# FFN input projection: Strassen-Winograd products for 19 of 22 pairs of gate and value blocks

## The chip, the cores and the metric

One core of one Trainium2 chip runs the whole program. The metric is the device time of one execution in microseconds (us). Engines: TensorE (PE; PEld is its weight load), VectorE (DVE), ScalarE (ACT), GpSimd (POOL) and SyncE (SP, which here only issues DMAs). Each works through its own list of instructions in order and waits for the others by semaphores.

## The reference, cut to what matters

The program is one inference step of a 4-layer decoder: 512 prompt positions and 8 sample tokens, 520 columns in all, width 1024. Every layer has a token mixer (NSA, gMLP, HGRN2, NSA) and then a SwiGLU FFN with 2816 hidden units, 22 blocks of 128:

```python
def deepnorm(x, h, g, b):
    return layer_norm(DEEPNORM_ALPHA * x + h, g, b)
def swiglu_ffn(x, w_in, w_out):
    gate, up = jnp.split(x @ w_in, 2, axis=-1)
    return (jax.nn.silu(gate) * up) @ w_out
```

Everything is float32. The FFN runs four times, once in each layer, on all 520 columns.

## The kernel before, in words

Activations lie transposed: x is 8 blocks of 128 features by 520 columns (tile `x`). A matrix product in near-float32 is made of three matmuls. `Split.put` and `Weights.conv` cut an operand into a rounded high part (an ACT cast to fp32r, L101 for weights, L210 for activations) and a low remainder (a DVE subtraction, L102 and L211), and `mm` adds up H*a, L*a and H*b for each block k of 128 features (L249, L250, L251). Columns go in two halves of 256 and 264 (`HS`), one PSUM bank each.

The 22 pairs of an FFN (a gate block and a value block of 128 hidden units) go in three chunks of 8, 7 and 7 (`CH`). In `ffn`, each pair and half takes two `mm` of 8 blocks (gate, value), then silu on ACT (L419), the product with the value on DVE (L420), and the split of the result (L210, L211). In the first chunk of a layer the first three pairs run their first halves, then their second ones, while the layer norm of the second half still runs; the other 19 go pair by pair. After a chunk, `out_proj` multiplies its hidden units by w_out, in 8 blocks of two halves, and adds to `x` (L382, L384). The last chunk's sums (L361, L363 on POOL) feed the layer norm.

Weights stream in one planned order for the whole kernel: SP's DMAs (L88) run `rawn` units ahead of the conversion, and conversion runs `ahead` = 2 units ahead of the matmuls. A unit is one block of 128 x 1024 and is converted at once by `conv`: two ACT casts and two DVE subtractions of 512 columns (half of the subtractions go to POOL in NSA). All big tiles come from one pool of 38 slots (`g`). Nothing reorders the program: each engine's list is in the order in which the Python code emits instructions.

## Time and profile before

| what | value |
|---|---|
| median of 3 runs | 3082.68 us (3077.68 to 3083.25) |
| the profiled execution: its own time | 3078.4 us |
| its span, first to last instruction | 3076.7 us |
| mean granted TensorE clock | 0.976 of full speed |
| busy share of the span | PE 94%, PEld 90%, DVE 56%, ACT 42%, POOL 15% |

The page's second part cuts the span into 40 slices; the granted clock (PEclk) reads 9 in each, that is 90% or more of full speed. The page's chain of waits, followed back from the end, spends 34% on PE, of which three times 10% are the lines L249 to L251. Two facts are needed to read the rows below. Matmuls are pipelined, so a matmul of 281 to 284 ns starts about every 0.12 us, and the time of a product is counted by how far apart later events lie, not by adding the matmuls' lengths. And a timeline row merges neighbours of one kind ("x4"): its second number then runs from the first start to the last end.

### The profile page before, as it was taken

How to read it: one execution, taken by the hardware profiler on the slowest of the kernel's cores; microseconds unless marked ns; L12 is line 12 of the kernel's file. 1: busy time of each engine (PE TensorE's matmuls, PEld its weight loads, DVE VectorE, ACT ScalarE, POOL GpSimd, SP SyncE). 2: the span in 40 equal slices, each digit the busy share in tenths (PEclk: the TensorE clock that was granted, in tenths of full speed). 3: DMA queues.
4: the chain of work that ended last, by engine and by line, in shares of the span. 5: the costliest groups of instructions: out<-in, count | busy, mean ns of one | idle time of the engine just before them, and what ended most of it. 6: DMA issues, size and time to landing. Idle time of an engine off the chain costs nothing. (4 is left out here: it accounts for less than half of the span.)

```text
span 3076.7 us, 56298 instructions
## 1 busy us (share of the span) xinstructions
PE 2886.1 (94%) x22730; PEld 2759.4 (90%) x22730; DVE 1725.9 (56%) x3821; ACT 1293.8 (42%) x2902; POOL 473.4 (15%) x446
## 2 busy tenths in 40 slices
PE   8889889999989999999999999999988998899997
PEld 8888569999989899998899889999888876799997
DVE  4888655333566633337677773333668876533334
ACT  4666534222355432234445543122456665432322
POOL 0222141000031200004222230000312222400002
PEclk9999999999999999999999999999999999999999
DMA  5212532223223222322222223223222244233221
GB/s 173 69 59 80 165 124 90 96 77 108 71 83 97 76 90 92 101 89 71 78 71 73 76 100 94 94 80 95 81 87 63 63 155 130 97 97 94 85 86 40
DMA packets 136039, 280.61 MB, mean 91 GB/s; under 512 B 13026, under 2 KB 76002, under 8 KB 135778
## 3 DMA queue, kind: packets, MB, share of 16 engines
q1 hardware_dynamic: 127168, 261.86, 26.8%
q10 hardware_dynamic: 7458, 10.95, 1.0%
q0 software_dynamic: 1152, 4.19, 0.5%
q8 instruction: 179, 2.93, 0.4%
q14 instruction: 82, 0.67, 0.1%
HBM read 263.69 MB, written 13.27 MB: 90 GB/s over the span
## 5 line engine op out<-in xcount | busy, mean ns | idle before, releaser
L249 PE MATMUL ps<-g 128*128 128x256 f32 (+1 forms) x6176 | 1784.8, 289 | 19.5 <-ACT g L101 12.9
L250 PE MATMUL ps<-g 128*128 128x256 f32 (+1 forms) x6176 | 1758.0, 285 | 10.9 <-DVE g L102 5.8
L251 PE MATMUL ps<-g 128*128 128x256 f32 (+1 forms) x6176 | 1759.1, 285 | 3.0 <-DVE g L211 1.7
L249 PEld LDWEIGHTS ps<-g 128*128 128x128 f32 x6176 | 1180.2, 191 | 34.6 <-ACT g L101 13.3
L250 PEld LDWEIGHTS ps<-g 128*128 128x128 f32 x6176 | 1179.7, 191 | 18.3 <-DVE g L102 7.1
L251 PEld LDWEIGHTS ps<-g 128*128 128x128 f32 x6176 | 1177.5, 191 | 4.6 <-DVE g L211 2.6
L102 DVE TENSOR_TENSOR g<-g 128x512 fp32r<-128x512 f32 (+1 forms) x708 | 467.6, 711 | 59.9 <-ACT g L101 52.5
L101 ACT CAST g<-g 128x512 fp32r<-128x512 f32 (+1 forms) x788 | 426.6, 608 | 105.4 <-DVE g L102 98.1
L420 DVE TENSOR_TENSOR row<-row,ps 128x256 f32<-128x256 f32 (+1 forms) x176 | 74.8, 425 | 515.8 <-PE ps L251 515.8
L210 ACT CAST g<-row 128x256 fp32r<-128x256 f32 (+1 forms) x192 | 78.6, 410 | 503.4 <-DVE row L420 491.7
L361 POOL TENSOR_TENSOR row<-x 128x256 f32<-128x256 f32 (+1 forms) x16 | 13.3, 834 | 1452.1 <-DVE x L384 1003.1
L419 ACT ACTIVATE row<-ps 128x256 f32<-128x256 f32 (+1 forms) x176 | 67.6, 384 | 334.3 <-PE ps L251 334.1
L952 ACT ACTIVATE g<-g,nst 128x128 f32<-128x128 f32 (+3 forms) x256 | 143.0, 559 | 128.0 <-DVE nst L950 123.9
L999 PE MATMUL ps<-g 128*128 128x512 f32 x384 | 142.1, 452 | 1.2 <-DVE g L987 0.9
L964 POOL TENSOR_SCALAR g<-g,nst 128x128 f32<-128x128 f32 (+3 forms) x64 | 76.4, 1193 | 414.8 <-DVE nst L957 345.4
L950 DVE CUSTOM_DVE_ANT_0 g<-ps,ncst 128x128 f32<-128x128 f32 (+3 forms) x256 | 119.3, 485 | 37.2 <-PE ps L948 27.8
L382 DVE SCALAR_TENSOR_TENSOR x<-x,ps 128x256 f32<-128x256 f32 (+1 forms) x128 | 52.9, 422 | 153.3 <-PE ps L251 153.1
L948 PE MATMUL ps<-g 128*128 128x256 f32 (+2 forms) x512 | 124.2, 346 | 13.9 <-DVE kcS L830 5.4
L102 POOL TENSOR_TENSOR g<-g 128x512 fp32r<-128x512 f32 x80 | 105.7, 1342 | 162.4 <-ACT g L101 147.6
L384 DVE TENSOR_TENSOR x<-x,ps 128x256 f32<-128x256 f32 (+1 forms) x128 | 53.8, 424 | 135.7 <-PE ps L251 135.6
L211 DVE TENSOR_TENSOR g<-row,g 128x256 fp32r<-128x256 f32 (+1 forms) x192 | 81.7, 429 | 83.8 <-ACT g L210 83.8
L316 POOL TENSOR_SCALAR x<-x,lngn,lngb 128x256 f32<-128x256 f32 (+1 forms) x120 | 104.8, 886 | 144.7 <-ACT g L312 129.9
(239 smaller groups left out, 2842.2 us busy)
## 6 DMA issues: line engine op xcount, KB each, us to landing
...
g<-cache_slc SPq DMA_DIRECT2D x128, 128.0 KB, 2.7
...
```

What stands on the lines that cost most here:

```text
L101: self.nc.scalar.copy(h[:, a:b], r[:, a:b])
L102: (self.sub[a > 0] or self.nc.vector).tensor_sub(l[:, a:b], r[:, a:b], h[:, a:b].bitcast(FT))
L210: self.nc.scalar.copy(h, src)
L211: self.nc.vector.tensor_sub(l, src, h.bitcast(FT))
L249: nc.tensor.matmul(p[:, :n], H[:, s], a, start=k == 0, stop=False)
L250: nc.tensor.matmul(p[:, :n], L[:, s], a, start=False, stop=False)
L251: nc.tensor.matmul(p[:, :n], H[:, s], b, start=False, stop=k == nk - 1)
L316: nc.gpsimd.tensor_scalar(xs[:, k], xs[:, k], g, b, op0=OP.mult, op1=OP.add)
L948: nc.tensor.matmul(p[:, :nn], q, kt[:, s, :nn], start=s == 0, stop=s == 1)
L950: nc.vector.tensor_tensor_reduce(P, p[:, :n], tri[:, 512 - n:], 1.0, 3e38, OP.add, OP.min, st[:, i:i + 1])
L952: defer(lambda P=P, i=i: (self.table(LN_EXP), nc.scalar.activation(P, P, AF.Exp, bias=st[:, i:i + 1], scale=-1.0, accum_out=st[:, 4 + i:5 ...
L999: nc.tensor.matmul(o, v, PT[:, s, :512], start=start and s == 0, stop=stop and s == 1)
```

## The change

Strassen's scheme in Winograd's form multiplies 2 x 2 blocks in seven products instead of eight. The left matrix A here is one pair: row 1 is the gate block and row 2 the value block, column c is the c-th half (512 values) of the 1024 features. The right matrix B is the activations: row r is the r-th half of the features, column c a half of 260 of the 520 columns. For 19 of the 22 pairs (`PLAIN` = 3 pairs stay as they were) `gated` runs seven products of four blocks k, with 12 matmuls of 260 columns each; before, a pair took 4 x 24 = 96 matmuls.

The left factors are A11, A12, A22 and four sums S1 = A21 + A22, S2 = S1 - A11, S3 = A11 - A21, S4 = A12 - S2. `Weights` now streams steps instead of units: a step is one 512-column factor, split into high and low by an ACT cast (now L141) and a DVE subtraction (now L142); `ahead` is 5 steps. The four sums of a pair are made on POOL (`sum`, 512 columns each). The right factors T1 to T4 are made once in each layer (`right`): subtractions on DVE and POOL, and their splits, run beside the second halves of the three plain pairs. The seven results are put together by DVE (L532, L540, L543, L549, each with one PSUM operand), ACT (L528, L535, and the two silu L538, L545) and POOL (L541, L546, L550). The splits of the hidden rows (`hid.put`, now L278 and L279) are emitted inside the next pair, after its first product.

All other weights are also converted in parts of 512 columns, each asked for where its first block k is used; the look-ahead of NSA is 3 parts (1 unit before). The first unit's conversion is no longer emitted in the middle of `setup`. NSA's small tiles and the FFN's new ones (`fsum`, `frow`) have pools that close after their phase; `SLOTS` is 39.

The diff, cut to its core:

```diff
 CH = (8, 7, 7)
+PLAIN = 3
...
-SLOTS = 38
+SLOTS = 39
...
+FACTORS = ("A11", "S2", "S1", "A12", "S3", "S4", "A22")
+SUMS = {4: "S1", 5: "S2", 6: "S3"}
+HALF = T // 2
...
-        self.rawn, self.ahead = 3, 2
...
+        self.rawn, self.ahead = 3, 5
...
+    def plan_pairs(self, pairs):
+        i0 = len(self.items)
+        for n, pair in enumerate(pairs):
+            i = len(self.items)
+            self.items.append(pair)
+            for q, name in enumerate(FACTORS):
+                early = SUMS.get(q) if n + 1 < len(pairs) else None
+                def step(i=i, q=q, name=name, early=early, first=n == 0):
+                    if q == 0:
+                        for x in ("S1", "S2", "S3", "S4") if first else ("S4",):
+                            self.sum(i, x)
+                    self.factor(i, name)
+                    if early:
+                        self.sum(i + 1, early)
+                self.add((i, name), step)
+        return list(range(i0, len(self.items)))
...
-    def conv(self):
-        i = self.ncv
-        n = self.src[i].shape[1]
-        r = self.raw.pop(i)
-        h, l = self.net.flat(FR), self.net.flat(FR)
-        c = (n // 256) * 128
-        for a, b in ((0, c), (c, n)):
-            self.nc.scalar.copy(h[:, a:b], r[:, a:b])
-            (self.sub[a > 0] or self.nc.vector).tensor_sub(l[:, a:b], r[:, a:b], h[:, a:b].bitcast(FT))
...
+    def split(self, key, src, eng):
+        n = src.shape[1]
+        t = self.net.flat(FR)
+        h, l = t[:, :n], t[:, 512:512 + n]
+        self.nc.scalar.copy(h, src)
+        (eng or self.nc.vector).tensor_sub(l, src, h.bitcast(FT))
+        self.ready[key] = h, l
...
+    def sum(self, i, name):
+        q = lambda r, c: self.quarter(i, r - 1, c - 1)
+        t = self.sums[i, name] = self.net.fsum()
+        g = self.nc.gpsimd
+        if name == "S1":
+            g.tensor_add(t, q(2, 1), q(2, 2))
+        elif name == "S2":
+            g.tensor_sub(t, self.sums[i, "S1"], q(1, 1))
+        elif name == "S3":
+            g.tensor_sub(t, q(1, 1), q(2, 1))
+        else:
+            g.tensor_sub(t, q(1, 2), self.sums[i, "S2"])
+    def factor(self, i, name):
+        if name[0] == "A":
+            src = self.quarter(i, int(name[1]) - 1, int(name[2]) - 1)
+        else:
+            src = self.sums.pop((i, name))
+        self.split((i, name), src, None)
+    def need(self, *key):
+        lim = min(len(self.steps), self.pos[key] + 1 + self.ahead)
+        while self.n < lim:
+            self.steps[self.n][1]()
+            self.n += 1
+        last = self.steps[lim - 1][0][0]
+        while self.nd < len(self.items) and self.nd <= last + self.rawn:
+            if sum(len(x) for x in self.items[last + 1:self.nd + 1]) > self.rawn:
+                break
...
+    def right(self, X, B):
+        nc = self.nc
+        x = lambda r, c, j: self.x[:, 4 * r - 4 + 2 * j:4 * r - 2 + 2 * j, HALF * (c - 1):HALF * c]
+        for n in ("T1", "T2", "T3", "T4"):
+            B[n] = [self.flat(FR)[:, :4 * HALF].rearrange("p (k t) -> p k t", k=4) for _ in range(2)]
+        for j in range(2):
+            t = {}
+            for n, o, p, q in (("T1", nc.vector, x(1, 2, j), x(1, 1, j)), ("T2", nc.vector, x(2, 2, j), "T1"),
+                               ("T3", nc.gpsimd, x(2, 2, j), x(1, 2, j)), ("T4", nc.gpsimd, "T2", x(2, 1, j))):
+                t[n] = self.fp.tile([128, HALF * 2], FT, name="fsum", tag="fsum", bufs=5).rearrange(
+                    "p (k t) -> p k t", k=2)
+                o.tensor_sub(t[n], t.get(p, p) if isinstance(p, str) else p, t[q] if isinstance(q, str) else q)
+                self.split(B[n][0][:, 2 * j:2 * j + 2], B[n][1][:, 2 * j:2 * j + 2], t[n])
+                yield
+        for r, c in ((1, 1), (2, 1), (2, 2)):
+            B[f"B{r}{c}"] = r, c
...
+    def prod(self, u, left, X, B, name, p, start=True):
+        nc = self.nc
+        H, L = self.W.need(u, left)
+        p = p[:, :HALF]
+        for k in range(4):
+            s = slice(k * 128, k * 128 + 128)
+            a, b = self.factor(X, B, name, k)
+            nc.tensor.matmul(p, H[:, s], a, start=start and k == 0, stop=False, skip_group_check=True)
+            nc.tensor.matmul(p, L[:, s], a, start=False, stop=False, skip_group_check=True)
+            nc.tensor.matmul(p, H[:, s], b, start=False, stop=k == 3, skip_group_check=True)
+            if k % 2:
+                self.tick()
...
+    def gated(self, u, X, B, out, last):
+        nc = self.nc
+        a, b, c, d = (None,) * 4
+        prod = lambda left, right, p, start=True: self.prod(u, left, X, B, right, p, start)
+        a = self.ps()
+        prod("A11", "B11", a)
+        s1, u2, s5, g0, u3, c21 = [self.frow() for _ in range(6)]
+        nc.scalar.copy(s1, a[:, :HALF])
+        out()
+        b = self.ps()
+        prod("S2", "T2", b)
+        nc.vector.tensor_add(u2, s1, b[:, :HALF])
+        c = self.ps()
+        prod("S1", "T1", c)
+        nc.scalar.copy(s5, c[:, :HALF])
+        prod("A12", "B21", a, False)
+        self.table(SILU)
+        nc.scalar.activation(g0, a[:, :HALF], AF.Silu)
+        prod("S3", "T3", b, False)
+        nc.vector.tensor_add(u3, s1, b[:, :HALF])
+        nc.gpsimd.tensor_add(s5, s5, u3)
+        prod("S4", "B22", c, False)
+        nc.vector.tensor_add(u2, u2, c[:, :HALF])
+        self.table(SILU)
+        nc.scalar.activation(u2, u2, AF.Silu)
+        nc.gpsimd.tensor_mul(u2, u2, s5)
+        d = self.ps()
+        prod("A22", "T4", d)
+        nc.vector.tensor_sub(c21, u3, d[:, :HALF])
+        (nc.vector if last else nc.gpsimd).tensor_mul(g0, g0, c21)
+        return u2, g0
 
...
             hid = Split(self)
-            g = {}
-            for j, h in self.order(n, 3 if c == 0 else 0, 0):
+            plain, pairs = u[2 * c]
+            m = len(plain) // 2
+            for j, h in self.order(m, m, 0):
                 c0, c1 = HS[h]
                 w = c1 - c0
-                pg = self.mm(u[2 * c][2 * j], 8, X, h)
-                pu = self.mm(u[2 * c][2 * j + 1], 8, X, h)
+                pg = self.mm(plain[2 * j], 8, X, h)
+                if h == 1 and right is None:
+                    right = self.spawn(self.right(X, B), 1)
+                pu = self.mm(plain[2 * j + 1], 8, X, h)
                 g = self.row()[:, :w]
                 self.table(SILU)
                 nc.scalar.activation(g, pg[:, :w], AF.Silu)
                 nc.vector.tensor_mul(g, g, pu[:, :w])
                 hid.put(j, c0, c1, g)
+            if right is not None:
+                run(right)
+            late = []
+            def out():
+                while late:
+                    late.pop(0)()
+            for j, pair in enumerate(pairs):
+                last = j == len(pairs) - 1
+                y1, y0 = self.gated(pair, X, B, out, last)
+                late.append(lambda j=m + j, y=y1: hid.put(j, HALF, T, y))
+                late.append(lambda j=m + j, y=y0: hid.put(j, 0, HALF, y))
+            out()
```

How each engine's list changes is seen in layer 0, at the second, third and fourth of the Strassen pairs (here A, B and C; before, any two neighbouring pairs). First VectorE, kernel before: L420 multiplies silu by the value, L211 splits the result, L102 splits weights.

```order
L420 TENSOR_TENSOR row_7330<-row_7330,ps_7305 128x256
L211 TENSOR_TENSOR g_7334<-row_7330,g_7333 128x256
L420 TENSOR_TENSOR row_7387<-row_7387,ps_7362 128x264
L211 TENSOR_TENSOR g_7334<-row_7387,g_7333 128x264
L102 TENSOR_TENSOR g_7393<-g_7177,g_7392 128x512 x2
L102 TENSOR_TENSOR g_7426<-g_7270,g_7425 128x512 x2
```

VectorE with the change, from the last result of A to the last but one of B. `frow_6111` and `frow_6113` are A's two hidden rows; `fsum_6141` is S4 of B, `fsum_6238` and `fsum_6218` are S2 and S1 of C.

```order
L549 TENSOR_TENSOR frow_6115<-frow_6114,ps_6214 128x260
L142 TENSOR_TENSOR g_6235<-fsum_6141,g_6235 128x512
L279 TENSOR_TENSOR g_6260<-frow_6111,g_6259 128x260
L279 TENSOR_TENSOR g_6260<-frow_6113,g_6259 128x260
L142 TENSOR_TENSOR g_6266<-g_6006,g_6266 128x512
L532 TENSOR_TENSOR frow_6253<-frow_6252,ps_6265 128x260
L142 TENSOR_TENSOR g_6287<-g_6146,g_6287 128x512
L142 TENSOR_TENSOR g_6309<-fsum_6238,g_6309 128x512
L142 TENSOR_TENSOR g_6325<-fsum_6218,g_6325 128x512
L540 TENSOR_TENSOR frow_6256<-frow_6252,ps_6265 128x260
L142 TENSOR_TENSOR g_6342<-g_6146,g_6342 128x512
L543 TENSOR_TENSOR frow_6253<-frow_6253,ps_6284 128x260
```

One split of 512 columns (S3 of C) follows before L549 of B. So a pair has 13 DVE instructions instead of 8, and nine of them read two SBUF tiles: seven weight splits and two splits of hidden rows, against four and two before.

POOL, kernel before, from the first layer norm of layer 0 (L316) to the sums of its FFN (L361, L363): between them, in all 22 pairs, POOL has nothing.

```order
L316 TENSOR_SCALAR x_67<-x_67,lngn_89,lngb_87 128x256 x4
L363 TENSOR_TENSOR row_4570<-row_4570,x_67 128x264 x4
L316 TENSOR_SCALAR x_67<-x_67,lngn_89,lngb_87 128x264 x8
L361 TENSOR_TENSOR row_9222<-x_67 128x256
L363 TENSOR_TENSOR row_9222<-row_9222,x_67 128x256 x5
```

POOL with the change, from A's last sums to B's: S1 of C stands ahead of A's last product (L550, which waits for L549), and S2, S3, S4 of C behind it.

```order
L541 TENSOR_TENSOR frow_6112<-frow_6112,frow_6114 128x260
L546 TENSOR_TENSOR frow_6111<-frow_6111,frow_6112 128x260
L158 TENSOR_TENSOR fsum_6218<-g_6148 128x512
L550 TENSOR_TENSOR frow_6113<-frow_6113,frow_6115 128x260
L160 TENSOR_TENSOR fsum_6238<-fsum_6218,g_6146 128x512
L162 TENSOR_TENSOR fsum_6269<-g_6146,g_6148 128x512
L164 TENSOR_TENSOR fsum_6285<-g_6146,fsum_6238 128x512
L541 TENSOR_TENSOR frow_6254<-frow_6254,frow_6256 128x260
L546 TENSOR_TENSOR frow_6253<-frow_6253,frow_6254 128x260
```

Seven two-operand instructions in each pair stand where there were none (in the last pair of a chunk L550 is on DVE, and there is no next pair to make sums for).

ScalarE with the change, from A's second silu (L545) to B's first (L538): the cast of S3 of B (`fsum_6125`) stands right behind the silu, and the casts of A's hidden rows (L278) behind B's first copy.

```order
L545 ACTIVATE frow_6111<-frow_6111 128x260
L141 CAST g_6215<-fsum_6125 128x512
L141 CAST g_6235<-fsum_6141 128x512
L528 COPY frow_6252<-ps_6234 128x260
L278 CAST g_6259<-frow_6111 128x260
L278 CAST g_6259<-frow_6113 128x260
L141 CAST g_6266<-g_6006 128x512
L141 CAST g_6287<-g_6146 128x512
L535 COPY frow_6254<-ps_6284 128x260
L141 CAST g_6309<-fsum_6238 128x512
L538 ACTIVATE frow_6255<-ps_6234 128x260
```

Before, a pair has two silu (L419), two casts of hidden rows (L210) and four casts of weights (L101) there; the casts no longer stand in one run of four.

## Rows read from the trace of the kernel before

**Rows 1.** Busy time in windows: PE, PEld, DVE, ACT, POOL, clock, DMA.

```profile
540.00:780.00 240.00, 240.00 (x2007) 240.00 (x2006) 86.64 (x169) 63.82 (x137) 0.00 (x0) 1.00 0.30 94
500.50:511.00 10.50, 10.50 (x89) 10.50 (x88) 1.73 (x4) 1.60 (x6) 0.00 (x0) 1.00 0.40 127
```

**Rows 2.** ACT timeline, two FFN pairs: start us, length us, instruction, wait before.

```profile
513.03 0.37 ACT L419 ACTIVATE row<-ps 128x256 f32<-128x256 f32 x1
...
522.10 0.41 ACT L210 CAST g<-row 128x264 fp32r<-128x264 f32 x1 [3.06 <-DVE row L420]
522.41 2.18 ACT L101 CAST g<-g 128x512 fp32r<-128x512 f32 x4
524.50 0.37 ACT L419 ACTIVATE row<-ps 128x256 f32<-128x256 f32 x1
...
536.01 0.38 ACT L419 ACTIVATE row<-ps 128x256 f32<-128x256 f32 x1
```

**Rows 3.** DVE timeline, the same pair.

```profile
523.07 2.50 DVE L102 TENSOR_TENSOR g<-g 128x512 fp32r<-128x512 f32 x4
527.30 0.42 DVE L420 TENSOR_TENSOR row<-row,ps 128x256 f32<-128x256 f32 x1 [1.74 <-PE ps L251]
528.19 0.43 DVE L211 TENSOR_TENSOR g<-row,g 128x256 fp32r<-128x256 f32 x1 [0.47 <-ACT g L210]
```

**Rows 4.** DVE timeline, end of FFN 0: one subtraction, then it with the next.

```profile
832.31 0.68 DVE L102 TENSOR_TENSOR g<-g 128x512 fp32r<-128x512 f32 x1
...
832.31 1.83 DVE L102 TENSOR_TENSOR g<-g 128x512 fp32r<-128x512 f32 x2
```

**Rows 5.** DVE timeline, the next subtraction alone.

```profile
832.91 1.22 DVE L102 TENSOR_TENSOR g<-g 128x512 fp32r<-128x512 f32 x1
```

**Rows 6.** POOL timeline, the same place.

```profile
832.54 1.05 POOL L363 TENSOR_TENSOR row<-row,x 128x256 f32<-128x256 f32 x1 [1.55 <-DVE x L384]
```

**Rows 7.** DVE timeline in NSA, layer 0.

```profile
172.51 0.42 DVE L1225 TENSOR_TENSOR g<-g 64x256 fp32r<-64x256 f32 x1
172.94 1.41 DVE L1226 TENSOR_TENSOR g<-g 64x256 fp32r<-64x256 f32 x1
```

**Rows 8.** POOL timeline, the same place: first subtraction.

```profile
172.63 1.44 POOL L102 TENSOR_TENSOR g<-g 128x512 fp32r<-128x512 f32 x1 [2.68 <-PE ps L948]
```

**Rows 9.** POOL timeline, second subtraction there.

```profile
174.03 1.44 POOL L102 TENSOR_TENSOR g<-g 128x512 fp32r<-128x512 f32 x1
```

**Rows 10.** POOL timeline, two such subtractions with DVE idle.

```profile
78.55 2.53 POOL L102 TENSOR_TENSOR g<-g 128x512 fp32r<-128x512 f32 x2 [61.15 <-ACT g L101]
```

**Rows 11.** DVE timeline, an instruction with a PSUM operand.

```profile
404.07 0.68 DVE L987 TENSOR_TENSOR g<-ps,g 128x512 fp32r<-128x512 f32 x1
```

**Rows 12.** POOL timeline beside it.

```profile
404.30 0.73 POOL L363 TENSOR_TENSOR row<-row,x 128x256 f32<-128x256 f32 x1 [3.34 <-DVE x L382]
404.99 1.27 POOL L102 TENSOR_TENSOR g<-g 128x512 fp32r<-128x512 f32 x1
```

**Rows 13.** POOL by line and form: count, busy us, mean ns.

```profile
L363 POOL TENSOR_TENSOR row<-row,x 128x264 f32<-128x264 f32 x40 | 30.2, 755 | 50.9 <-DVE x L384 33.4 <-DVE x L382 16.5
```

**Rows 14.** The page's groups of matmuls: idle time before, its releaser.

```profile
L249 PE MATMUL ps<-g 128*128 128x256 f32 (+1 forms) x6176 | 1784.8, 289 | 19.5 <-ACT g L101 12.9
L250 PE MATMUL ps<-g 128*128 128x256 f32 (+1 forms) x6176 | 1758.0, 285 | 10.9 <-DVE g L102 5.8
```

**Rows 15.** PE timeline, the first matmul.

```profile
10.85 0.58 PE L249 MATMUL ps<-g 128*128 128x256 f32 x1 [10.85 <-ACT g L101]
```

94 lines of the change are left out of this document (62 added, 32 removed).

## The prediction, on record before the run

> **What bounds the kernel now.** I read the busy windows first, to see which engine never rests inside the FFN; then the timelines of ACT and DVE, for the length of one pair and for what the other engines do in it; then places where DVE and POOL work at once, because the change gives POOL work in the FFN for the first time; last the page's groups, for waits on weights. In the FFN, PE and its weight loads are busy in every one of 240 us, at a granted clock of 1.00 (2.4 GHz), DVE for 86.64 us, ACT for 63.82 us, POOL not at all [rows 1]. The first silu of two successive pairs starts at 513.03, 524.50 and 536.01 us [rows 2]: a pair takes 11.49 us. It has 96 matmuls, so one takes 11.49 / 96 = 119.7 ns. Nothing waits on PE's side; DVE waits for PE (1.74 us ahead of L420 in [rows 3]). So in the FFN only fewer matmuls help, as long as the other engines keep up.
>
> **What the change removes.** Seven products of 12 matmuls are 84 in place of 96. Columns are 260, the mean of 256 and 264, so I keep 119.7 ns: 84 x 119.7 = 10.05 us a pair, 1.44 us less. 76 pairs change (19 in each of 4 layers): 109 us, if PE stays the bound. Of that I now take off what DVE and POOL give back.
>
> **What it adds, engine by engine.** ACT, per pair: seven casts at 2.18 / 4 = 0.55 us, two silu at 0.38, two casts of hidden rows at 0.41 [rows 2], and two copies out of PSUM at no more than the silu's 0.38: 6.2 us of 10.05. DVE: seven splits at 0.60 (four take 2.50 us, [rows 3], the first of them 0.68, [rows 4]), two splits of hidden rows at 0.43, four instructions with a PSUM operand at 0.42: 6.8 us. POOL: four sums at 1.27 [rows 10, 12] and three short ones at 0.755 [rows 13]: 7.35 us. Each alone fits into 10.05 us.
>
> Together they don't, and this is the step that sets my forecast. DVE's L102 at 832.91 us takes 1.22 us, where its neighbour takes 0.68; a POOL addition of 256 columns ends inside it, at 833.59 [rows 4 to 6]. In NSA a DVE subtraction of 256 columns takes 1.41 us, its like before it 0.42; it ends 0.28 us after the end of the POOL subtraction at 174.07, and POOL's next one, two of which alone take 2.53 us, ends 1.12 us after DVE's end [rows 7 to 10]. An instruction of DVE that reads a PSUM operand keeps its 0.68 us beside POOL [rows 11, 12]. So where both read two SBUF tiles, the two engines take turns. By those ends a turn costs: DVE 512 columns 834.14 - 833.59 = 0.55 us, DVE 260 columns 0.28; POOL 512 columns 1.12; POOL 256 columns 833.59 - 832.99 = 0.60, which I keep for 260. A pair's turns: DVE 7 x 0.55 + 2 x 0.28 = 4.41, POOL 4 x 1.12 + 3 x 0.60 = 6.28, in all 10.69 us. That is above PE's 10.05, and below 11.49. If the turns hid nothing of an instruction's start and end, the recorded lengths would add: DVE 7 x 0.68 + 2 x 0.43 = 5.62, POOL 7.35, in all 12.97 us. These are the ends of the unknown pace of a pair in mid-chunk, with 10.05 below if turns cost nothing.
>
> To choose between them I lay one pair B out in the order of the lists, each engine in order, a free turn going to the engine that waited first. At 0 DVE ends L549 of A, while POOL's S1 runs until 0.75. DVE splits S4 (1.30); POOL multiplies L550 (1.90); DVE puts the first hidden row (2.18); POOL S2 (3.30); the second row, whose cast had to wait for L550 (3.58); POOL S3 (4.70); split A22 (5.25); POOL S4 (6.37), beside it L532; splits of A11, S2 and S1 (6.92, 7.52, 8.12); L540 (8.54); split A12 (9.14), then POOL's L541 (9.74) and beside it L543 (9.56). The cast of S3 stands behind the silu in ACT's list: 9.6 + 0.38 + 0.55 makes 10.5; POOL's L546, behind the same silu, has the turn until 10.8; split of S3 (11.35), L549 of B (11.77). POOL's next S1 then runs 0.70 us on, so the pattern closes, at 11.7 us. L549's hidden row, POOL's sums and PE hang on this chain: product S3 reuses the bank that L532 reads, so PE waits for L532 and can't run more than two products ahead. One swapped turn is worth up to 0.55 us either way, and a chain in strict turns is the less favourable order; I take 11.4 us, between the sum of turns and the layout and nearer to the latter.
>
> Not every pair is in mid-chunk. The first of a chunk finds its sums made under the products before it and has no hidden rows of a neighbour to split; the second one uses up the two products' lead; the last has no sums to make for a next one, and works off the backlog. I give three pairs in each of 12 chunks PE's pace: 36 pairs at 10.05. The rest, four in each of 8 chunks of seven and two in each of 4 chunks of five, are 40 pairs at 11.4. Gain: 36 x 1.44 + 40 x 0.09 = 51.8 + 3.6 = 55 us.
>
> **The other edits.** The right factors: in each layer 4 subtractions and 8 splits on DVE and 4 subtractions on POOL, in turns 12 x 0.55 + 4 x 1.12 = 11 us. They stand beside the second halves of the plain pairs, from the first gate on five `mm` of 24 matmuls, 14.4 us, where DVE is now busy for 1.73 of 10.5 us [rows 1]. That covers them; if the cover were gone it would be 11 us a layer, 44 in all. I take 2 us a layer, 8 in all, since S1 to S4 of the first pair are queued on POOL just ahead of them. ACT's 8 casts (4.4 us) have the same cover. Weights in parts of 512 columns instead of 1024, everywhere: it touches only waits on splits, which are 12.9 us behind ACT's L101 and 5.8 us behind DVE's L102 [rows 14], and 10.85 of the former are the start of the kernel [rows 15]. So it can give at most 8 us; a loss of the same size is possible where a part now comes late, as at the start, where the first unit is converted behind two more splits of x. I take 0. DMAs keep number and size; a pair is fetched as two tiles at once, with 4 products, 5.7 us, ahead of its first sum. Small pools and one more slot: 0, nothing waits for them in a list above.
>
> Sum: 3078.4 (the profiled execution; span 3076.7) - 55 + 8 = 3031. That execution lies 4.3 us under the median of the runs shown, which would make 3036. I forecast 3033 us.
>
> **Rivals.** (1) PE stays the bound, because the five steps of look-ahead hide the turns: the gain is 109 - 8 = 101 us, 2977; with a pair at the sum of turns, 10.69, it is 36 x 1.44 + 40 x 0.80 - 8 = 76, 3002. For it: no engine is over 7.4 us alone. Against it: 10.69 already exceeds PE's time, and L532 ties PE to DVE's list.
>
> (2) Slower: DVE and POOL exclude each other for whole instructions, and a pair in mid-chunk takes 12.97 us. Place: VectorE's splits and POOL's sums. 36 x 1.44 - 40 x 1.48 - 8 = -15: 3094. It decides from the pace at which 40 x (pace - 11.49) eats 51.8 - 8 us: 12.6 us. For it: DVE's 1.22 and 1.41 us, and some fourteen handovers in a pair, to which the layout gives no delay. Against it: the measured turns of 0.55 and 1.12 are shorter than the lengths of 0.68 and 1.27, so the starts do overlap. The Trainium skill ("SBUF — State Buffer", section "Who interferes with whom") states the rule behind this rival: a DVE instruction with two SBUF inputs contends with a GpSimd instruction that reads SBUF, and whoever is second "fully blocks" until the first has finished. The trace agrees that the two never run together [rows 4 to 9]; taken by whole recorded lengths, the rule would make it the 3094 us of this rival, by the ends measured here the turns of the forecast.
>
> (3) It comes out even: what is won at the chunks' ends is lost to the right factors (44 instead of 8 us) at a pace of 11.7: 51.8 - 8.4 - 44 = 0. For it: POOL's T3 and T4 stand behind five sums. Against it: the cover of 14.4 us. About 3078.
>
> **Chances.** Forecast, a pace of 10.9 to 12.3, 3010 to 3068: 0.58. Rival 1, 2970 to 3005: 0.18. Rival 2: 0.16. Rival 3: 0.08. A measurement can tell about 0.2%, 6 us, from no change. Faster: 0.58 + 0.18 less a little for the forecast's slow end, 0.74; the same 0.09; slower 0.17. The likeliest case's own range is 3010 to 3068; the range for 8 in 10 takes in most of rival 1 and part of rival 2: 2982 to 3088.
>
> **What would show it.** Starts of silu L538 in neighbouring pairs: 10.05 us apart at a chunk's start, 11.4 in the middle. DVE's splits (L142) at a mean near 1 us instead of 0.69, POOL's sums at 1.4 or more. PE waiting in the FFN for DVE's L532, and for hardly anything else there. If the pairs are 10.1 us apart throughout, the turns were no bound and rival 1 holds; over 12.6, rival 2. PE's matmuls 119.7 ns apart within a product show the first term. If time is won or lost outside the gated products by over 8 us, my zero for the parts of 512 columns was wrong.

## The result and the profile after

The changed kernel takes 3124.55 us (median of 4 runs, 3123.52 to 3125.63) against 3080.35 us for the kernel before on the same chip: a ratio of 1.0143, with an interval of 1.0126 to 1.0161. I had forecast 3033 us and a range up to 3088; it is slower by 1.4%, and outside the range. The profiled span grew from 3076.7 to 3123.4 us, by 46.7.

I cut both spans at the first update of `x` in each `out_proj` (L382 or L384 before, L450 or L452 after), which gives a table by stage:

| stretch, us | before | after | change | I had predicted |
|---|---|---|---|---|
| NSA of layer 0 | 382.9 | 383.2 | +0.3 | 0 |
| four first chunks of the FFNs, together | 659.4 | 698.6 | +39.2 | -10 |
| eight chunks of seven pairs, together | 987.0 | 979.1 | -7.9 | -37 |
| gMLP | 170.2 | 174.1 | +3.9 | 0 |
| HGRN | 398.3 | 412.7 | +14.4 | 0 |
| NSA of layer 3, end | 478.9 | 475.7 | -3.2 | 0 |

(Predicted: per chunk of seven 3 x 1.44 + 4 x 0.09 = 4.7 us; per first chunk 3 x 1.44 + 2 x 0.09 - 2 = 2.5.) So three things went another way: the pairs in the middle of a chunk, the start of each FFN (the largest part: 49 of the 94 us by which the stretches differ from the forecast), and HGRN, which has no gated products at all. The 3.2 us in NSA of layer 3 are not clear of noise: in runs whose NSA is the changed kernel's this stretch reads 473.5 to 479.6, and 478.9 lies within that.

The changed kernel's page, busy time by engine:

```profile
PE 2817.0 (90%) x21818; PEld 2672.3 (86%) x21818; DVE 2210.6 (71%) x4261; ACT 1487.5 (48%) x3314; POOL 1169.2 (37%) x982
```

There are fewer matmuls, and PE is no longer always at work. Its busy windows, columns as in [rows 1]: the stretch that is shown there, the first gated pair of FFN 0, and part of HGRN.

```profile
540.00:780.00 240.00, 226.86 (x1868) 224.28 (x1866) 166.23 (x242) 98.49 (x212) 121.70 (x95) 1.00 0.30 92
515.00:530.00 15.00, 10.93 (x74) 10.52 (x74) 11.15 (x17) 8.12 (x19) 7.72 (x7) 0.89 0.22 70
1522.00:1672.00 150.00, 135.68 (x1058) 133.66 (x1058) 112.75 (x206) 71.97 (x150) 34.03 (x18) 0.92 0.21 69
```

PE rests for 13 of the 240 us in which it never rested before, DVE's busy time has nearly doubled, and POOL works half of the time. In the other two windows the granted clock is below 1 as well; in the kernel before it reads 1.00 in both.

**A pair in the middle of a chunk.** The changed kernel's ACT timeline, the first silu of four neighbouring pairs, which answers to [rows 2]:

```profile
626.56 0.39 ACT L538 ACTIVATE frow<-ps 128x260 f32<-128x260 f32 x1 [0.55 <-PE ps L513]
636.62 0.39 ACT L538 ACTIVATE frow<-ps 128x260 f32<-128x260 f32 x1 [0.24 <-PE ps L513]
648.28 0.39 ACT L538 ACTIVATE frow<-ps 128x260 f32<-128x260 f32 x1
660.03 0.39 ACT L538 ACTIVATE frow<-ps 128x260 f32<-128x260 f32 x1
```

The starts are 10.06, 11.66 and 11.75 us apart; in all twelve chunks the steps settle at 11.74 to 11.89. The first step is 84 x 119.7 ns, as predicted. The others are longer than the 11.49 us of the eight products, at a granted clock of 1.00. What PE waits for there, by its view of waits (what waits, for what: us in total, times, longest):

```profile
PE ps L511 <- DVE frow L532: 75.0, 52, 1.5
```

L532 reads the bank into which the product S3 T3 is to be added, and it stands late in DVE's list. DVE's timeline for one such pair:

```profile
655.31 0.41 DVE L549 TENSOR_TENSOR frow<-frow,ps 128x260 f32<-128x260 f32 x1
655.64 1.44 DVE L142 TENSOR_TENSOR g<-fsum,g 128x512 fp32r<-128x512 f32 x1
657.01 0.97 DVE L279 TENSOR_TENSOR g<-frow,g 128x260 fp32r<-128x260 f32 x1
658.17 1.25 DVE L279 TENSOR_TENSOR g<-frow,g 128x260 fp32r<-128x260 f32 x1 [0.19 <-ACT g L278]
659.34 1.78 DVE L142 TENSOR_TENSOR g<-g 128x512 fp32r<-128x512 f32 x1
661.04 0.41 DVE L532 TENSOR_TENSOR frow<-frow,ps 128x260 f32<-128x260 f32 x1
...
666.28 0.90 DVE L142 TENSOR_TENSOR g<-fsum,g 128x512 fp32r<-128x512 f32 x1 [1.00 <-ACT g L141]
667.10 0.41 DVE L549 TENSOR_TENSOR frow<-frow,ps 128x260 f32<-128x260 f32 x1
```

And POOL's, beside it:

```profile
654.79 1.74 POOL L158 TENSOR_TENSOR fsum<-g 128x512 f32<-128x512 f32 x1
656.50 1.19 POOL L550 TENSOR_TENSOR frow<-frow 128x260 f32<-128x260 f32 x1
657.65 1.48 POOL L160 TENSOR_TENSOR fsum<-fsum,g 128x512 f32<-128x512 f32 x1
659.09 1.48 POOL L162 TENSOR_TENSOR fsum<-g 128x512 f32<-128x512 f32 x1
660.53 1.74 POOL L164 TENSOR_TENSOR fsum<-g,fsum 128x512 f32<-128x512 f32 x1
```

Read the ends, counted from the end of L549 at 655.72: POOL's S1 at 0.81, DVE's split 1.36, POOL's L550 1.97, the first hidden row 2.26, S2 3.41, the second row 3.70, S3 4.85, the split of A22 5.40, S4 6.55. My layout had 0.75, 1.30, 1.90, 2.18, 3.30, 3.58, 4.70, 5.25 and 6.37. The two engines take strict turns, in the order that I had laid out. The rest of the pair follows the layout too: the split of S3 ends at 11.46 and L549 of the next pair at 11.79, where the layout has 11.35 and 11.77. So DVE's list is the pair: DVE is busy for 10.56 of the 11.75 us between two silu starts, and waits 1.00 and 0.19 us for casts of ACT. The recorded lengths hold the waiting for a turn: DVE's forms, mean ns of one after the busy time, against 0.68 and 0.43 us in [rows 3, 4]:

```profile
L142 DVE TENSOR_TENSOR g<-g 128x512 fp32r<-128x512 f32 x568 | 535.3, 955 | 122.5 <-ACT g L141 118.8
L279 DVE TENSOR_TENSOR g<-frow,g 128x260 fp32r<-128x260 f32 x152 | 139.2, 916 | 16.2 <-ACT g L278 14.6
L532 DVE TENSOR_TENSOR frow<-frow,ps 128x260 f32<-128x260 f32 x76 | 31.5, 414 | 0.0
```

and POOL's, against 1.27 us [rows 10, 12]:

```profile
L158 POOL TENSOR_TENSOR fsum<-g 128x512 f32<-128x512 f32 x76 | 123.8, 1629 | 163.1 <-DMA g<-ffn_in 163.1
```

L532, which has a PSUM operand, keeps its length.

**The start of an FFN.** The changed kernel's PE timeline at the first gated pair of FFN 1:

```profile
1095.34 0.28 PE L513 MATMUL ps<-g 128*128 128x260 f32 x1
1102.61 0.59 PE L511 MATMUL ps<-g 128*128 128x260 f32 x1 [6.99 <-ACT frow L528]
1102.99 0.42 PE L512 MATMUL ps<-g 128*128 128x260 f32 x1
1103.21 0.42 PE L513 MATMUL ps<-g 128*128 128x260 f32 x1
```

PE waits 7 us for L528, the copy of the first product out of PSUM (3.1 us in FFN 0, 1.5 in FFN 2 and 3); after the wait matmuls start 0.22 us apart in place of 0.12, the lower of the clock's two levels (1.2 GHz). Over the four first chunks the granted clock reads 0.95, 0.96, 0.94 and 0.95, against 0.96, 0.99, 0.99 and 0.96 before; no run tells the share of the clock from that of the waits. ACT's timeline shows why the copy is late:

```profile
1092.86 0.63 ACT L278 CAST g<-fsum 128x520 fp32r<-128x520 f32 x1 [0.28 <-POOL fsum L489]
1093.39 0.38 ACT L578 ACTIVATE row<-ps 128x264 f32<-128x264 f32 x1
1096.07 0.41 ACT L278 CAST g<-row 128x264 fp32r<-128x264 f32 x1 [2.30 <-DVE row L579]
...
1099.17 1.28 ACT L401 ACT_TABLE_LOAD   x1
...
1102.19 0.37 ACT L528 COPY frow<-ps 128x260 f32<-128x260 f32 x1
```

The last cast of the right factors ends at 1093.49; the silu of the plain pairs, a side job of FFN 1 with two table loads, and only then L528 follow in the list.

**HGRN.** PE's waits for the level products in it, before, and after:

```profile
PE ps L646 <- ACT g L630: 14.2, 15, 1.8
```

```profile
PE ps L819 <- ACT g L803: 24.0, 11, 3.1
```

Fewer but longer waits, and a clock of 0.92 in the window shown above. DVE's timeline in the changed kernel, ahead of one of 3 us:

```profile
1570.06 1.77 DVE L789 TENSOR_TENSOR g<-g 128x512 f32<-128x512 f32 x1
1571.76 2.38 DVE L142 TENSOR_TENSOR g<-g 128x512 fp32r<-128x512 f32 x1
1574.06 2.38 DVE L801 TENSOR_TENSOR g<-g 128x512 f32<-128x512 f32 x1
```

A split of a weight's second part stands between two steps of the chain that PE waits for, and takes 2.38 us.

### The profile page after: what moved, and what is told of

The parts are those of the page before. It is cut to its first block, busy times and chain, and to the rows that moved or that the text cites. A ratio compares the mean times of both kernels' runs of the same rounds, so it can differ in the third digit from the quotient of the medians.

```text
span 3123.4 us, 56467 instructions
## 1 busy us (share of the span) xinstructions
PE 2817.0 (90%) x21818; PEld 2672.3 (86%) x21818; DVE 2210.6 (71%) x4261; ACT 1487.5 (48%) x3314; POOL 1169.2 (37%) x982
## 4 chain that ended last, share of the span: by engine, by line
PE 48%; DVE 25%; ACT 10%; POOL 7%; issue 7%; DMA 2%; SPq 0%; ACTq 0%; DVEq 0%; POOLq 0%
PE ps L319 10%; PE ps L317 10%; PE ps L318 10%; DVE g L142 8%; PE ps L511 3%; PE ps L513 3%; PE ps L512 3%; POOL frow L550 2%; DVE row L362 2%; POOL fsum L158 2%; PE ps L819 1%; POOL x L384 1%; ACT g L1128 1%; ACT g L278 1%; DVE g L1126 1%
## 5 line engine op out<-in xcount | busy, mean ns | idle before, releaser
L317 PE MATMUL ps<-g 128*128 128x256 f32 (+1 forms) x3744 | 1103.2, 295 | 22.0 <-ACT g L141 13.7
L319 PE MATMUL ps<-g 128*128 128x256 f32 (+1 forms) x3744 | 1076.7, 288 | 9.3 <-DVE g L340 7.8
L318 PE MATMUL ps<-g 128*128 128x256 f32 (+1 forms) x3744 | 1073.7, 287 | 10.7 <-DVE g L142 8.0
L317 PEld LDWEIGHTS ps<-g 128*128 128x128 f32 x3744 | 725.8, 194 | 37.1 <-ACT g L141 13.9
L318 PEld LDWEIGHTS ps<-g 128*128 128x128 f32 x3744 | 725.1, 194 | 17.6 <-DVE g L142 8.8
L319 PEld LDWEIGHTS ps<-g 128*128 128x128 f32 x3744 | 722.7, 193 | 13.2 <-DVE g L340 8.8
L511 PE MATMUL ps<-g 128*128 128x260 f32 x2128 | 611.9, 288 | 93.8 <-DVE frow L532 75.0
L142 DVE TENSOR_TENSOR g<-g 128x512 fp32r<-128x512 f32 (+1 forms) x632 | 569.7, 919 | 122.5 <-ACT g L141 118.8
L513 PE MATMUL ps<-g 128*128 128x260 f32 x2128 | 605.6, 285 | 3.0 <-DVE g L279 3.0
L512 PE MATMUL ps<-g 128*128 128x260 f32 x2128 | 605.2, 284 | 0.0
L511 PEld LDWEIGHTS ps<-g 128*128 128x128 f32 x2128 | 405.1, 190 | 106.4 <-DVE frow L532 85.8
L141 ACT CAST g<-g 128x512 fp32r<-128x512 f32 (+1 forms) x712 | 407.4, 607 | 93.2 <-DVE g L142 50.2
L513 PEld LDWEIGHTS ps<-g 128*128 128x128 f32 x2128 | 405.5, 191 | 3.9 <-DVE g L279 3.9
L512 PEld LDWEIGHTS ps<-g 128*128 128x128 f32 x2128 | 405.4, 191 | 0.0
L142 DVE TENSOR_TENSOR g<-fsum,g 128x512 fp32r<-128x512 f32 x304 | 262.9, 881 | 85.4 <-ACT g L141 85.3
L141 ACT CAST g<-fsum 128x512 fp32r<-128x512 f32 x304 | 180.2, 614 | 77.9 <-PE ps L319 38.4
L142 POOL TENSOR_TENSOR g<-g 128x512 fp32r<-128x512 f32 x80 | 105.6, 1326 | 251.0 <-ACT g L141 245.6
L541 POOL TENSOR_TENSOR frow<-frow 128x260 f32<-128x260 f32 x76 | 79.1, 1041 | 288.3 <-DVE frow L540 288.3
L158 POOL TENSOR_TENSOR fsum<-g 128x512 f32<-128x512 f32 x76 | 123.8, 1629 | 163.1 <-DMA g<-ffn_in 163.1
L384 POOL TENSOR_SCALAR x<-x,lngn,lngb 128x256 f32<-128x256 f32 (+1 forms) x120 | 105.1, 888 | 155.9 <-ACT g L380 142.8
```

The lines of the kernel that those rows point to most:

```text
L141: self.nc.scalar.copy(h, src)
L142: (eng or self.nc.vector).tensor_sub(l, src, h.bitcast(FT))
L158: g.tensor_add(t, q(2, 1), q(2, 2))
L317: nc.tensor.matmul(p[:, :n], H[:, s], a, start=k == 0, stop=False)
L318: nc.tensor.matmul(p[:, :n], L[:, s], a, start=False, stop=False)
L319: nc.tensor.matmul(p[:, :n], H[:, s], b, start=False, stop=k == nk - 1)
```

## The experiments

All are compared with the kernel before on the same chip, in us. The columns are sums of the stretches of the first table. Some of the expectations below cut the stages at other places (there HGRN is 388.0 us before and 401 in the changed kernel); compare their changes with the table's, not their lengths. The runs e2_nosum, e6_noT, e8_unused and e14_apart leave work out or feed other numbers to the same matmuls, so they are no versions to use.

| run | first chunks | chunks of seven | HGRN | median, us | ratio to before |
|---|---|---|---|---|---|
| before | 659.4 | 987.0 | 398.3 | 3080.35 | 1 |
| changed | 698.6 | 979.1 | 412.7 | 3124.55 | 1.0143 (1.0126 to 1.0161) |
| e1_plain | 664.2 | 986.8 | 410.6 | 3095.54 | 1.0055 (1.0035 to 1.0075) |
| e2_nosum | 656.2 | 911.2 | 410.8 | 3015.04 | 0.979 (0.9764 to 0.9816) |
| e8_unused | 707.6 | 979.4 | 411.9 | 3135.13 | 1.0179 (1.0158 to 1.02) |
| e14_apart | 712.7 | 955.8 | 410.7 | 3111.87 | 1.0111 (1.0085 to 1.0137) |
| e4_all_dve | 669.0 | 929.4 | 410.7 | 3043.18 | 0.988 (0.9858 to 0.9901) |
| e5_units | 691.2 | 979.1 | 397.1 | 3103.35 | 1.0077 (1.0058 to 1.0096) |
| e6_noT | 667.3 | 975.8 | 410.9 | 3089.01 | 1.0035 (1.0024 to 1.0047) |
| e7_Tpipe | 693.1 | 979.4 | 411.9 | 3120.85 | 1.0133 (1.0116 to 1.015) |
| e15_bounds | 697.8 | 983.6 | 411.3 | 3127.20 | 1.0161 (1.0133 to 1.0189) |
| e9_comb | 660.5 | 924.4 | 397.2 | 3016.72 | 0.9794 (0.9778 to 0.9811) |
| e10_pool3 | 658.9 | 922.0 | 397.9 | 3008.37 | 0.9764 (0.9748 to 0.978) |
| e11_mul | 663.4 | 940.7 | 399.2 | 3035.26 | 0.9849 (0.9833 to 0.9866) |
| e12_plain4 | 666.2 | 940.5 | 395.8 | 3039.88 | 0.9859 (0.9842 to 0.9876) |
| e13_pool3_plain4 | 659.7 | 923.0 | 397.4 | 3014.15 | 0.9788 (0.9772 to 0.9805) |
| e16_best | 656.3 | 924.5 | 397.2 | 3009.45 | 0.9776 (0.9755 to 0.9796) |

### Theory and rivals

Theory: the loss is three separate things, turns of DVE and POOL in every pair, the right factors at the start of each FFN, and the conversion by parts outside the FFN. Rivals: in the pairs, a wait for data (for POOL's sums, or for PSUM banks) rather than turns; at the start, the first pair's sums and the slots; in HGRN, something that the FFN ahead of it leaves behind.

### The side edits alone: e1_plain

```diff
-            m = PLAIN if c == 0 else 0
+            m = n
```

> All 22 pairs by eight products again, no right factors; the weights still come in parts of 512 columns, with 39 slots and NSA's own pool. Theory (the side edits cost by themselves): the FFN stages are back within 2 us of before (392.7, 391.4, 392.4, 391.1), gMLP stays near 177, HGRN near 401 against 388.0, NSA stays 2 to 4 us below before; the whole about 3090 (3084 to 3098). Rival (HGRN loses only because of the FFN ahead of it, the parts cost nothing): HGRN near 388, the whole at 3073 to 3082.

HGRN is at 410.6 (+12.3) and gMLP at 174.1 (+3.9) without a single gated product. The first chunks are 4.8 us longer, the chunks of seven as before. The side edits alone cost 0.55%; I had put them at zero.

### The order of the parts: e5_units

```diff
-        lim = min(len(self.steps), self.pos[key] + 1 + self.ahead)
+        lim = min(len(self.steps), self.pos[(key[0], 0) if key[1] == 1 else key] + 1 + self.ahead)
```

> As the changed kernel, but both 512-column parts of a weight block are split when its first part is wanted, as before; the gated products are untouched. Theory (HGRN and gMLP lose because the split of each second part lands half a block later in ScalarE's and VectorE's lists): HGRN back at 388 to 391, gMLP at 174 to 175, the whole 3104 to 3113. Rival (HGRN's loss comes from something else, as the slots or the granted clock after the FFN): HGRN stays at 398 or more, the whole 3119 to 3128.

Both parts of a block are converted again where its first part is wanted. HGRN is at 397.1, 1.2 us below before, and gMLP at 172.1 (174.1 in the changed kernel); the whole is 3103.35, at the lower end of what I expected. DVE's timeline in e5_units at the place shown above:

```profile
1561.75 1.82 DVE L789 TENSOR_TENSOR g<-g 128x512 f32<-128x512 f32 x1
1563.68 2.20 DVE L801 TENSOR_TENSOR g<-g 128x512 f32<-128x512 f32 x1
```

No split stands between the two steps. The window of HGRN in e5_units:

```profile
1522.00:1672.00 150.00, 141.56 (x1146) 137.12 (x1147) 112.67 (x205) 74.14 (x156) 36.29 (x20) 0.99 0.27 85
```

The clock is back at 0.99, and PE's waits in HGRN are short ones again:

```profile
PE ps L819 <- ACT g L803: 16.4, 17, 2.0
```

So the rival falls: the gated products ahead of HGRN are still there.

### What makes a pair 11.8 us: e2_nosum, e8_unused, e14_apart

```diff
-            src = self.sums.pop((i, name))
+            src = self.quarter(i, *{"S1": (1, 0), "S2": (0, 0), "S3": (0, 1), "S4": (1, 1)}[name])
```

and in e2_nosum the calls of `self.sum` are gone, in e8_unused they stay. e14_apart is e8_unused with L541, L546 and L550 on `nc.vector`.

> The four sums on GpSimd of each pair are left out: the products that want S1 to S4 take the hi/lo of a raw quarter of the block, so other numbers are computed by the same matmuls. Theory (GpSimd's sums and VectorE's splits take turns, and this makes the mid-chunk pair 11.8 us): pairs in the middle of a chunk start 10.05 to 10.3 us apart, the splits of 512 columns on VectorE fall from 0.95 to about 0.6 us, and some 52 pairs give back 1.5 us each: 3040 to 3055. Rival (the order of ScalarE's copies, or the PSUM banks, sets the pace): pairs stay above 11.3 us, the whole above 3105.

> The sums S1 to S4 are made on GpSimd as in the changed kernel, but nobody reads them: the products that want them take raw quarters of the block (other numbers, the same matmuls). So GpSimd's time is no longer in the chain of any product; only its being at work beside VectorE is left. Theory (the two engines hold each other up): mid-chunk pairs stay at 11 us or more, a split of 512 columns on VectorE at 0.9 us or more, the whole 3090 to 3115. Rival (what counts is that products wait for GpSimd's sums): pairs at 10.0 to 10.3 us, as without the sums, the whole 3010 to 3030.

> GpSimd makes S1 to S4 of every pair and nobody reads them, as before; now the three short operations behind the matmuls are on VectorE too, so that neither a product nor a hidden row waits for GpSimd, directly or through its list (other numbers, the same matmuls). Theory (the two engines hold each other up while both read SBUF): VectorE has 7 x 0.60 + 4 x 0.36 + 3 x 0.35 + 2 x 0.34 = 7.4 us a pair of its own, and GpSimd's four sums hold it up for up to 4 x 1.12 us: mid-chunk pairs at 10.6 to 11.6 us, a split of 512 columns on VectorE at 0.85 us or more. Rival (in the run where the sums were unused, pairs were long because VectorE waited for rows of GpSimd's list): pairs at 10.05 to 10.2 us as without the sums, splits at 0.75 or less.

Without the sums the pairs run at PE's pace: 10.02 to 10.11 us in all chunks of seven. The whole is 3015.04 us, below the 3040 to 3055 that I expected, because the first chunks gain too (see below). Two silu starts in e2_nosum, and its splits:

```profile
659.60 0.39 ACT L533 ACTIVATE frow<-ps 128x260 f32<-128x260 f32 x1 [0.55 <-PE ps L508]
669.65 0.39 ACT L533 ACTIVATE frow<-ps 128x260 f32<-128x260 f32 x1 [0.55 <-PE ps L508]
```

```profile
L137 DVE TENSOR_TENSOR g<-g 128x512 fp32r<-128x512 f32 x872 | 643.0, 749 | 259.2 <-ACT g L136 250.0
```

With the sums made but used by nobody (e8_unused) the pairs are 11.8 us again, and PE's wait is the same as in the changed kernel:

```profile
PE ps L512 <- DVE frow L533: 74.5, 52, 1.5
```

This run did not settle it, against what I wrote ahead of it: the hidden rows still came from POOL, behind the sums. The whole, 3135.13 us, is above the range that I gave for either case; its first chunks are 9 us longer than the changed kernel's, and those of e14_apart 14 us, and no run here shows why. In e14_apart nothing within a pair waits for POOL, and SyncE's waits for POOL's sums are 0.2 us in all. Two silu starts there, and its splits:

```profile
642.64 0.39 ACT L539 ACTIVATE frow<-ps 128x260 f32<-128x260 f32 x1
653.95 0.39 ACT L539 ACTIVATE frow<-ps 128x260 f32<-128x260 f32 x1
```

```profile
L142 DVE TENSOR_TENSOR g<-g 128x512 fp32r<-128x512 f32 x872 | 776.0, 909 | 136.3 <-ACT g L141 129.1
```

The steps of a chunk of seven are uneven now: about 11.2 to 11.9, 11.4, 10.5, 11.3 and 11.3 us, and 10.05 for the last, near the theory's 10.6 to 11.6 and not the rival's 10.05 to 10.2; the six make 65.6 to 66.6 us, against about 68.9 in the changed kernel and 60.4 in e2_nosum. Splits take 909 ns in place of 749, on average over all stages. In e4_all_dve below DVE makes the same sums itself, in its own list, and its six steps make 62.9. One step of each, columns as in [rows 1], first e14_apart, then e4_all_dve:

```profile
642.64:653.95 11.31, 10.34 (x84) 10.13 (x84) 10.76 (x18) 5.60 (x15) 5.81 (x4) 1.00 0.27 92
639.54:650.19 10.65, 10.33 (x84) 10.12 (x84) 10.01 (x21) 5.90 (x13) 0.00 (x0) 1.00 0.34 102
```

DVE has the four sums less to do in e14_apart and is busy for longer: that POOL is at work beside DVE costs a pair more than all its work costs on DVE. So it is the turns; what waits for POOL's results adds the rest, up to 11.8. The Trainium skill ("SBUF — State Buffer", section "Who interferes with whom") names this contention; these runs agree that the two engines exclude each other, but taken by whole recorded lengths the rule would have been 12.97 us a pair, and the trace has 11.8: the measurement decides.

### Without POOL in the pairs: e4_all_dve

```diff
-        g = self.nc.gpsimd
+        g = self.nc.vector
```

This is in `sum`; L541, L546 and L550 go to `nc.vector` in the same way.

> The four sums of a pair and the three short sums and products behind its matmuls go to VectorE, GpSimd has nothing in the gated products. Theory (turns, not the amount of work): alone VectorE needs 0.42 us for a split or sum of 512 columns, so 11 x 0.42 + 2 x 0.28 + 4 x 0.41 + 3 x 0.28 = 7.7 us a pair, under TensorE's 10.05; mid-chunk pairs start 10.05 to 10.5 us apart and the whole is 3030 to 3055, chunk 0 of every FFN still some 10 us late. Rival (VectorE's list becomes the bound, every add that frees a bank queues behind the sums): pairs at 11 us or more, the whole above 3085.

81 us under the changed kernel and 1.2% under the one before; the whole lies in the range that I gave, the pace of the pairs does not. Chunks of seven give back 49.7 us. My sum for DVE was too low: 0.42 us is the length for 260 columns, a split of 512 takes 0.60 also alone [rows 3], and the pairs settle at 10.65 us, not at PE's 10.05. The first chunks are only 9.6 us over before, all four together; I had expected some 10 us each.

### The first chunks: e6_noT, e7_Tpipe, e15_bounds

e6_noT leaves out the sums and splits in `right`. e7_Tpipe:

```diff
-                o.tensor_sub(t[n], t.get(p, p) if isinstance(p, str) else p, t[q] if isinstance(q, str) else q)
-                self.split(B[n][0][:, 2 * j:2 * j + 2], B[n][1][:, 2 * j:2 * j + 2], t[n])
+                nc.vector.tensor_sub(t[n], t.get(p, p) if isinstance(p, str) else p, t[q] if isinstance(q, str) else q)
+                nc.scalar.copy(h, t[n])
+                late.append((l, t[n], h.bitcast(FT)))
+                if len(late) > 1:
+                    nc.vector.tensor_sub(*late.pop(0))
...
-                    right = self.spawn(self.right(X, B), 1)
+                    right = self.spawn(self.right(X, B), 2)
```

e15_bounds moves `self.spawn(self.bounds())` of FFN 1 from its first to its second chunk.

> As the changed kernel, but the sixteen sums and splits of the right factors T1 to T4 are left out: the products that want a T take the rows of X instead (other numbers, the same matmuls), and the eight slots stay held. Theory (the chain of the right factors holds ScalarE's and VectorE's lists over the first gated pair): the first chunk's stretch falls from 195.3 to 188 to 190 in FFN 0, from 162.2 to 151 to 154 in FFN 1, 145 to 137 to 139 and 196 to 188 to 191 in FFN 2 and 3; the whole 3085 to 3100. Rival (the first pair's sums on GpSimd and the slots are what is late): the stretches stay within 2 us, the whole above 3114.

> As the changed kernel, but the right factors are formed in another order: all sums on VectorE, each low part one step behind its high part, twice the emission rate. Theory (the chain is long because each step waits for the one before it on another engine): it ends some 5 us earlier, each first chunk gives back 4 to 7 us, the whole 3098 to 3110. Rival (the amount of work, not its order, holds the lists): unchanged, 3118 to 3128.

> As the changed kernel, but the gate bounds of HGRN, a side job of FFN 1 with two table loads on ScalarE, start with its second chunk instead of its first. Theory (in the first chunk of FFN 1 they stand behind the right factors and ahead of the first gated pair's copy, and make its stall 7 us in place of 3.3): the stall falls to 3 to 4 us, the first chunk of FFN 1 from 162.2 to 156 to 159. Rival (the stall is the right factors' alone): unchanged within 1.5 us.

Without the right factors' work the four first chunks fall by 4.5, 11.4, 7.4 and 8.1 us, 31.4 together, with the slots still held, and the stalls for L528 are gone. In FFN 0 the stretch came to 190.8, a little over the 188 to 190 expected.

That is what the right factors cost beside POOL's sums, and not a loss apart from the sums. e2_nosum keeps the right factors and leaves the sums out, and its first chunks fall by 42.4 us, to 656.2. About 20 of these lie in the steps between the gated pairs (four steps of a first chunk make 45.5 to 46.4 us in the changed kernel, 40.4 to 41.7 in e2_nosum), about 23 ahead of the first silu of the gated pairs. The wait for L528's place in FFN 1 is shorter there, but not gone (the copy is L523 in that file):

```profile
1072.56 0.59 PE L506 MATMUL ps<-g 128*128 128x260 f32 x1 [4.78 <-ACT frow L523]
```

Ahead of that silu e6_noT gives back about 34 us and has no stall left at the first gated pair; e2_nosum gives back about 23. So the rival of e6_noT, the first pair's sums, holds a part: about two thirds of what the start loses is lost only where the right factors and the sums meet.

The other order of e7_Tpipe brings 5.5 us over the four, near the rival: it is mostly the amount of work, not its order. In e15_bounds the wait for L528 in FFN 1 falls from 7 to 1.5 us, the one ahead of it, for a cast of the right factors, grows from 0.7 to 2.1, and the first chunk of FFN 1 is 3.7 us shorter, as expected; but the second is 4.4 longer. (The first chunk of FFN 0, which this edit does not touch, differs by 2.7 us between the two profiles, so the waits say more here than the lengths.) PE's longest wait for L532 in that second chunk is 3.8 us: the side job has its price there too. So it does make up part of FFN 1's 7 us, and moving it gains nothing.

### Together: e9_comb, e10_pool3, e11_mul, e12_plain4, e13_pool3_plain4, e16_best

e9_comb has the edits of e4, e5 and e7, and `out()` behind L532's add; e10_pool3 puts L541, L546 and L550 back on POOL; e11_mul is e9_comb with

```diff
-        nc.vector.tensor_mul(u2, u2, s5)
         d = self.ps()
         prod("A22", "T4", d)
+        nc.vector.tensor_mul(u2, u2, s5)
```

e12_plain4 is e11_mul with `PLAIN = 4`, e13 is e10 with it, e16 is e10 with the edit of e15.

> Together: the pair's sums and short operations on VectorE (alone 81 us under the changed kernel), both parts of a block split at its first (alone 21 us under it), the right factors in the other order, and the splits of the last pair's outputs placed behind the add that frees the second bank. Theory (these are separate losses, and the 0.6 us a pair that is left with the sums on VectorE is that add's place in the list): mid-chunk pairs 10.05 to 10.3 us, first chunks 4 to 7 us shorter, HGRN 388, the whole 2975 to 3000. Rival (VectorE is simply full in these pairs): pairs stay at 10.6, the whole 3008 to 3025.

> As the combination, but the three short operations of 260 columns behind the matmuls of a pair are on GpSimd again; the sums of 512 columns stay on VectorE. Theory (VectorE is full in a mid-chunk pair of the combination: 11 x 0.60 + 4 x 0.36 + 3 x 0.35 + 2 x 0.34 + 0.5 of waiting = 10.3 to 10.7; the three take 1.05 and the wait from it, and three short turns of GpSimd cost it less than that): mid-chunk pairs 10.05 to 10.3 us, the whole 2990 to 3004. Rival (any GpSimd work between the two reads costs what it saves): pairs at 10.6 or more, the whole 3012 to 3025.

> As the combination, but the product of the second silu stands behind the matmuls of the last product in the program, so that the splits and the sum these ask for come ahead of it on VectorE, which waited 0.49 us there for ScalarE's silu. Theory (VectorE's list is the bound of the pair, and every idle moment in it counts): mid-chunk pairs 10.15 to 10.3 us, the whole 2992 to 3004. Rival (the bound is elsewhere): pairs at 10.6, the whole 3014 to 3020.

> As the run with the product moved, and four pairs of each first chunk by eight products in place of three. Theory (in the first chunk VectorE has not time enough for the sixteen sums and splits of the right factors and the first pair's four sums while TensorE does three plain pairs; a fourth gives TensorE 11.5 us of work and costs 1.5 us): the stalls at the first gated pair (2.9 and 1.5 us in FFN 0, 5.8 and 0.6 in FFN 1) go, FFN 0 and 1 are 2 to 5 us shorter, FFN 2 and 3 up to 1.5 us longer, the whole 2 to 9 us less than with three. Rival (the stalls move to the new first gated pair): the whole 4 to 7 us more than with three.

> As the run with the three short operations on GpSimd, and four plain pairs in each first chunk in place of three: the same gain or loss as the fourth plain pair brings in the other run, 2 to 9 us less than with three by the theory, 4 to 7 us more by the rival.

> The combination with the three short operations on GpSimd (3008 us) and the bounds of HGRN in the second chunk of FFN 1. Theory: the stall of 5.8 us there falls to about 3, the whole 3003 to 3008. Rival: unchanged, 3006 to 3013.

The combination is 2.1% faster than before, but the early add only frees the second and third step of a chunk; then the pairs are 10.65 us apart again, as the rival said, and the whole, 3016.72, lies in the rival's range. With the three short operations on POOL they are 10.5, between theory and rival, and the whole is 3008.37 us, 2.4% faster than before: the lowest median of all runs, though its interval still touches that of e9_comb. e11_mul was a miss: pairs of 11.0 us, and 18.5 us slower than e9_comb. DVE's idle time says why. Its wait in a pair of e9_comb (one more, of 0.08 us, is not shown):

```profile
653.96 0.43 DVE L552 TENSOR_TENSOR frow<-frow 128x260 f32<-128x260 f32 x1 [0.49 <-ACT frow L551]
```

and in e11_mul, where it had been expected to vanish:

```profile
652.64 0.69 DVE L142 TENSOR_TENSOR g<-fsum,g 128x512 fp32r<-128x512 f32 x1 [1.00 <-ACT g L141]
```

The cast behind the silu in ACT's list is what DVE then waits for, and that is half a microsecond later still. The list plus its waits is the pair: DVE is busy for 10.00 of 10.63 us in e9_comb, and for 9.91 of 10.97 in e11_mul. A fourth plain pair moves the stall to that pair's own weights, with a wait of 4.2 to 4.4 us in each of the four FFNs. PE's timeline in e12_plain4:

```profile
496.82 0.38 PE L317 MATMUL ps<-g 128*128 128x256 f32 x1 [4.25 <-ACT g L141]
```

The medians are 4.6 us higher in e12_plain4 than in e11_mul and 5.8 higher in e13_pool3_plain4 than in e10_pool3, but the intervals overlap: a fourth plain pair gains nothing, against the theory, and that it costs something, as the rival said, is not clear of noise. e16_best is e10_pool3 within what can be told apart.

## Why the prediction was wrong, point by point

- **PE bounds the FFN before, and 84 matmuls take 10.05 us.** Right: 10.02 to 10.09 us at the first step of a chunk of seven, and 10.02 to 10.11 at every one in e2_nosum.
- **DVE and POOL take turns.** Right, and the layout was right to 0.2 us at every end that I compared; the signs that I had named came too (splits at 0.955 us, POOL's sums at 1.5 to 1.66, PE waiting for L532). **"I take 11.4 us" failed:** I discounted the layout's 11.7 (its last step reads 11.77) because a chain in strict turns seemed the less favourable order. The measured pace is 11.8, a loss against 11.49 instead of a gain.
- **"I give three pairs in each of 12 chunks PE's pace" failed.** Only the first step of a chunk of seven runs at PE's pace; the second is already 11.6, and in the first chunks even the first step takes 10.3 to 11.2. The six steps of a chunk of seven make 1.43 - 0.17 - 4 x 0.32 = 0 us; the 1.1 us that its stretch gains (126.1 to 125.0) are won around its last pair. I had 4.7. These two errors are 37.4 - 7.9 = 29.5 us of the miss in the chunks of seven. In the first chunks I had counted 18 us of gain on the pairs by the same two steps, and there too the steps make 45.5 to 46.4 us, against 4 x 11.49 = 46.0.
- **"I take 2 us a layer" for the right factors failed.** Beside POOL's sums their work costs 31.4 / 4 = 7.9 us a layer (e6_noT), not 2; I had 11 without cover, so little of it was covered. I had named the sums queued on POOL as the reason for the 2, so the place was right and the size was not. I read the cover from a window in which DVE was busy for 1.73 of 10.5 us [rows 1], in a kernel whose DVE did not yet split the first gated pair's factors there. In e9_comb, where DVE does all of it without POOL, it works from 494.10 to 509.69 us with hardly a gap (15.05 of 15.59 us). What was due behind it in ACT's list, L528, I did not look for.
- **"I take 0" for the parts of 512 columns failed.** 16 us in HGRN and gMLP (e1_plain), twice the bound that I gave. I had bounded it by PE's waits on splits [rows 14]. But a split is paid for also by what stands behind it in DVE's list: HGRN's chain waited for it.
- **The rivals.** Rival 2 had the sign but not the pace (12.97); its slower result at 3094 lies 30 us under the measured one. Rival 3 named two of the terms that did fail, the right factors and 11.7 us; I gave it 0.08.

What remains open: after e6_noT the first chunks are still 7.9 us over before. Part of it is the side edits (4.8 in e1_plain); part is a wait of about 2 us in each layer for the layer norm's last split, which is 1.1 or less in e1_plain. It is not the sums' doing alone, since e2_nosum has it too (1.1 to 2.1 us); no run here shows its cause. Also in the fastest version the first chunks take as long as before (658.9), so that their twenty gated pairs gain nothing.
